# A decoder layer on one core: first weight block, norm tables and block inverse re-ordered

## The chip, the core and the metric

The kernel runs on one core of a Trainium2 chip. The core has TensorE (PE, matrix products, with its weight loads as PEld), VectorE (DVE), ScalarE (ACT), GpSimd (POOL) and SyncE (SP), each with a list of instructions of its own that it works through in order; between engines, semaphores say when an operand is ready. Transfers are issued from the lists of SP, ACT and POOL and carried out by 16 transfer engines. The metric is the device time of one execution in microseconds (us), as the median of several runs.

## The reference

One layer over 256 positions, 2048 channels, all in float32:

```python
h = rmsnorm(x, norm1_g)
qkv, z, b_raw, a_raw, u_raw, v_raw, ga_raw, gb_raw = split(h @ w_in)
# branch A: causal conv + silu on qkv, l2norm of q and k, then the gated delta rule in chunks of 64
L    = strict_lower(k_beta @ k.T * decay)
Tinv = triangular_solve(L + eye, eye)          # per head and chunk, 64 x 64
u = Tinv @ v_beta;  w = Tinv @ (k_beta * exp(g))   # then a scan over 4 chunks with state S
y_a = rmsnorm(o, dn_onorm_g) * silu(z)
# branch B: spatial gating
u  = gelu(u_raw)
vg = layernorm(gelu(v_raw), sg_ln_g, sg_ln_b)
ws = tril(sg_w)                                 # 8 groups of 128 x 128
y_b = u * (ws @ vg + sg_b)
merged = sigmoid(ga_raw) * (y_a @ w_branch_a) + sigmoid(gb_raw) * (y_b @ w_branch_b)
x = x + merged @ w_out
h2 = rmsnorm(x, norm2_g)
x = x + (silu(causal_dwconv(h2 @ ffn_w_gate) + ffn_conv_b) * (h2 @ ffn_w_up)) @ ffn_w_down
out = rmsnorm(x, final_norm_g)
```

## The kernel before

**Dense products.** Every weight matrix is streamed from memory once. A weight block (four slabs of 128 rows by up to 512 columns) is transferred to a `w_raw` buffer, of which there are three. Two slabs at a time, `split` makes a rounded high half `w_hi` (a cast on ACT, L123) and the remainder `w_lo` (a subtraction on DVE, L124); of each half there are four buffers. The activations are held as high and low halves too (`x_h`), and `tok_mms` issues three products per slab and row tile: high by high (L150), high by `w_lo` (L151), low by high (L152). With two row tiles and two slabs a step has twelve products. So PE follows ACT's cast and DVE's subtraction, and they follow PE through the four buffers.

**Stages.** First `vg_pass` computes the columns of v, with input slabs that are scaled and split on the way (L206, L207). Its first block comes in single slabs: g1, x_t and `w_raw` are transferred from SP and ACT. Then the square sums of x (ACT, L318, on tiles `xn`) give the row factors: `rs_v` on DVE (L286), a power on POOL (L287), two diagonal tiles `dg` on DVE, their products `ps_row` on PE (L297), and a copy `rrow` on ACT. In the stage of branch B, ACT applies Gelu to the four v tiles (L337), DVE takes their statistics and normalises them: one instruction per row tile for mean and deviation, and eight half-tile instructions in `affine` for gain and bias. Meanwhile PE computes three groups of u columns (`ps_u`). `sg_w` is loaded as `ws`, masked to its lower triangle on POOL (L382) and transposed on PE (`ps_ws`). Then follow q, k, v, the delta rule of branch A with gates, branch B's projection and z between its steps, the merge, and the feed-forward part, which takes the greater half of the time.

**The order.** The program is a list of operations in Python; generators decide which small operations are written between which dense steps. `affine` yields after each piece, and every second yield lets one dense step of u in. `delta()` yields numbers of dense steps (`fill_steps`: gates, branch B's projection, z), which the loop at the end of the stage takes from the other generator. `inverse_base` solves the 16 by 16 diagonal blocks row by row (L610, L613 on DVE, i from 1 to 15), and yields 2 after every fourth row. A scheduler then places the operations of all engines in an order of its own, by readiness, so that the lists of the engines need not follow the Python order.

Of the kernel before, what the change touches and what calls it, by code (L numbers as in the profile page):

```python
# [16 lines left out]
P = 128  # L17
# [81 lines left out]
def decoder_kernel(ctx: ExitStack, tc: tile.TileContext, a: dict):  # L99
# [15 lines left out]
        return ap.bitcast(F32)  # L115


    def split(raw, shape, tag, dst=None):

        hi, lo = dst or (  # L120
            wsp.tile(shape, F32R, name=f"w_{n}", tag=tag + n)[..., 0 : raw.shape[-1]] for n in ("hi", "lo")
        )
        nc.scalar.copy(hi, raw)  # L123
        nc.vector.tensor_tensor(lo, raw, f32(hi), op=ALU.subtract)  # L124
        return hi, lo

# [107 lines left out]
    def vg_pass():  # L234

        ps = [[bank(pool, "ps_vg") for _ in range(NT)] for pool in (acc, aux)]
        for kb in range(0, NK, 4):
            raws = [wraw.tile([P, 4, 512], F32, name="w_raw", tag="raw") for _ in range(2)]
            n = 2 if kb else 1
            for j in range(0, 4, n):  # L240
                k0 = kb + j
                for c, raw in enumerate(raws):
                    at = P * 512 * (c * NK + kb)
                    block = a["w_vg"][at : at + P * 4 * 512].rearrange("(p k n) -> p k n", p=P, n=512)
                    if k0 == 0 and c == 0:
                        nc.sync.dma_start(g1, a["par"][:, 96:112])
                    if c == 0:
                        queue = nc.sync if k0 else nc.scalar
                        queue.dma_start(x_t[:, k0 : k0 + n, :], a["xt"][:, k0 : k0 + n, :])
                    queue = nc.scalar if k0 == 0 and c else nc.sync  # L250
                    queue.dma_start(raw[:, j : j + n, :], block[:, j : j + n, :])
                if k0 == 0:
                    nc.scalar.copy(tbl, tbl)
                for k in range(k0, k0 + n):
                    split_stat(x_h[:, k, 0:T], x_h[:, k, T:], x_t[:, k, :], g1[:, k : k + 1])
                for c, raw in enumerate(raws):
                    hi, lo = split(raw[:, j : j + n, :], [P, n, 512], "w")
                    tok_mms(ps[c], x_h, NK, k0, n, hi, lo)
        return ps

# [64 lines left out]
    with tc.tile_pool(name="sg", bufs=1) as sg:  # L325
        ln_g = sg.tile([P, SGW], F32, name="ln_g")
        ln_b = sg.tile([P, SGW], F32, name="ln_b")
        nc.gpsimd.dma_start(ln_g, a["sg_ln_g"].partition_broadcast(P))
        nc.gpsimd.dma_start(ln_b, a["sg_ln_b"].partition_broadcast(P))
        vg = sg.tile([P, NT, SGW], F32, name="vg")  # L330
        st = sg.tile([P, NT, 2, 6], F32, name="st")
        ws = sg.tile([P, NG, P], F32, name="ws")
        ws_t = sg.tile([P, NG, P], F32, name="ws_t")
        for c in range(2):
            for t in range(NT):
# [6 lines left out]
            nc.vector.bn_aggr(mv[:, t, :], st[:, t].rearrange("p c s -> p (c s)"))  # L342
        rs = sg.tile([P, NT], F32, name="sg_rs")
        rsqrt_small(rs, mv[:, :, 1], 1.0)
        for t in range(NT):
            nc.vector.tensor_scalar(
                vg[:, t, :], vg[:, t, :], scalar1=mv[:, t, 0:1], scalar2=rs[:, t : t + 1],
                op0=ALU.subtract, op1=ALU.mult,
            )

        def affine():

            for t in range(NT):
                for gain, op in ((ln_g, ALU.mult), (ln_b, ALU.add)):
                    for q in range(2):
                        qs = slice(512 * q, 512 * (q + 1))
                        nc.vector.tensor_tensor(vg[:, t, qs], vg[:, t, qs], gain[:, qs], op=op)
                        yield

        ug = sg.tile([P, NT, SGW], F32, name="ug")  # L360
        for c, (start, width) in enumerate(GROUPS["bau"]):
            steps = tok_steps(x_h, source("bau", c), NK, "ps_u_")
            if c == 0:
                next(steps)
                next(steps)
                for i, _ in enumerate(affine()):
                    if i % 2:
                        next(steps)
            ps = finish(steps)
            n0 = max(0, C_U - start)  # L370
            u0 = start + n0 - C_U
            for t in range(NT):
                if n0:
                    nc.vector.tensor_scalar(
                        ba[:, t], ps[t][:, 0:n0], scalar1=rstd1[:, t : t + 1], scalar2=None, op0=ALU.mult
                    )
                nc.scalar.activation(
                    ug[:, t, u0 : u0 + width - n0], ps[t][:, n0:], AF.Gelu, scale=rstd1[:, t : t + 1]
                )
            if c == 0:  # L380
                nc.gpsimd.dma_start(ws, a["sg_w"].rearrange("g i j -> i g j"))
                nc.gpsimd.affine_select(  # L382
                    ws, ws, pattern=[[0, NG], [-1, P]], compare_op=ALU.is_ge, fill=0.0, base=0, channel_multiplier=1
                )
                for q in range(2):
                    pw = bank(aux, "ps_ws")
                    for g in range(4):
                        nc.tensor.transpose(pw[:, g * P : (g + 1) * P], ws[:, 4 * q + g, :], cm["ident"])
                    nc.scalar.copy(ws_t[:, 4 * q : 4 * q + 4, :], pw.rearrange("p (g i) -> p g i", g=4))
                continue  # L390
            for t in range(NT):
                uh = ug[:, t, 512 * (c - 1) : 512 * c]
                pm = bank(aux, "ps_mix")
                for g in range(4):
                    gg = 4 * (c - 1) + g
                    gs = slice(g * P, (g + 1) * P)
                    nc.tensor.matmul(
                        pm[:, gs], lhsT=ws_t[:, gg, :], rhs=vg[:, t, gg * P : (gg + 1) * P], start=True, stop=True
                    )
                for g in range(4):  # L400
                    gg = 4 * (c - 1) + g
                    gs = slice(g * P, (g + 1) * P)
                    nc.vector.scalar_tensor_tensor(
                        uh[:, gs], pm[:, gs], sgbt[:, gg : gg + 1], uh[:, gs], op0=ALU.add, op1=ALU.mult
                    )
                to_chan(uh, y_b, t, 4 * (c - 1))
# [181 lines left out]
    def inverse_base(lows):  # L588
# [19 lines left out]
        for i in range(1, BASE):  # L608
            pr = dnt.tile([P, 2, BASE, BASE], F32, name="pr", tag="w_sb")[:, :, 0:i, 0:i]
            nc.vector.tensor_tensor(  # L610
                pr, bc(lt[:, :, 0:i, i], 2, i), xs[:, :, 0:i, 0:i].rearrange("p b j c -> p b c j"), op=ALU.mult
            )
            nc.vector.tensor_reduce(xs[:, :, i, 0:i], pr, axis=AX.X, op=ALU.add)  # L613
            if i % 4 == 3:
                yield 2
        res = []
        for n, order in (("x_i", "p b i j -> p j b i"), ("x_it", "p b i j -> p i b j")):
            xc = dnt.tile([P, BASE, 32], F32, name="xc", tag="w_sb")
# [383 lines left out]
```

## Time and profile before

| | |
|---|---|
| runs (median of 3; lowest, highest) | 1433.55 us; 1433.12, 1434.66 |
| profiled execution, its span | 1434.71 us; 1432.8 us |
| PE busy | 1418.1 us (99%) |
| DVE, ACT, POOL busy | 895.9, 718.3, 228.4 us |
| transferred | 269.19 MB, 188 GB/s mean |
| granted clock of TensorE | 0.87 in the first 10 us, 0.95 in the next, then 1.00 |

Times in the rows of a timeline are the start from the span's beginning, then the duration; a row of a group ends with how many instructions it holds, and in brackets stands how long the engine had been idle before it and what ended that. In a row of waits, the engine and its instruction stand left of the arrow, what released it stands right of it, and the numbers are the total, how often, and the longest. The durations of products overlap: the pace is the difference of two starts.

### The profile page before, as it was taken

What the parts mean: (1) busy time and instruction counts of PE and PEld (TensorE: products, weight loads), DVE (VectorE), ACT (ScalarE), POOL (GpSimd) and SP (SyncE); (2) the same over time, 40 slices, a digit from 0 to 9 for tenths busy, and PEclk for the clock granted to TensorE, in tenths of its full rate; (3) what the DMA queues carried; (4) which work ended last, traced back from release to release, by engine and by line L of the source; (5) the groups of instructions that cost most, each with busy time, mean ns of one, the idle gap of its engine ahead of it and who ended that gap; (6) DMA issues with size and microseconds to landing.
All of it is one profiled execution on the core that took longest, in us unless ns stands there. A gap on an engine that the chain in (4) does not pass through costs nothing.

```text
span 1432.8 us, 19529 instructions
## 1 busy us (share of the span) xinstructions
PE 1418.1 (99%) x7768; PEld 1208.2 (84%) x7768; DVE 895.9 (63%) x1121; ACT 718.3 (50%) x977; POOL 228.4 (16%) x216
## 2 busy tenths in 40 slices
PE   9999999999999999999999999999999999999997
PEld 7998888887888888888888888888888888888886
DVE  5666777779465645656566675766766666555555
ACT  6546556543333444445465555555555545444443
POOL 0101111221011200200031221322312221000002
PEclk9999999999999999999999999999999999999999
DMA  7864555545334455575555555555555555555552
GB/s 262 298 216 158 212 191 177 176 147 188 137 120 145 157 196 181 177 286 179 180 183 196 197 185 193 189 183 199 179 204 179 198 183 203 182 202 189 193 199 95
DMA packets 46011, 269.19 MB, mean 188 GB/s; under 512 B 4832, under 2 KB 11744, under 8 KB 16096
## 3 DMA queue, kind: packets, MB, share of 16 engines
q1 hardware_dynamic: 44912, 264.93, 52.5%
q0 software_dynamic: 432, 1.57, 0.4%
q8 instruction: 61, 1.00, 0.3%
q10 hardware_dynamic: 576, 1.44, 0.3%
q14 instruction: 30, 0.25, 0.0%
HBM read 265.83 MB, written 2.10 MB: 187 GB/s over the span
## 4 chain that ended last, share of the span: by engine, by line
PE 90%; DVE 3%; POOL 1%; issue 1%; ACT 0%; POOLq 0%; DVEq 0%
PE ps_gu L183 23%; PE ps_gu L186 11%; PE ps_qkv L183 6%; PE ps_dn L895 5%; PE ps_dn L896 5%; PE ps_dn L894 5%; PE ps_gate L150 4%; PE ps_gate L151 4%; PE ps_gate L152 3%; PE ps_qkv L186 3%; PE ps_wo L150 2%; PE ps_wo L152 2%; PE ps_wo L151 2%; PE ps_br L151 2%; PE ps_br L150 2%; PE ps_br L152 2%
## 5 line engine op out<-in xcount | busy, mean ns | idle before, releaser
L124 DVE TENSOR_TENSOR w_lo<-w_raw,w_hi 128x1024 fp32r<-128x1024 f32 (+3 forms) x412 | 529.7, 1291 | 361.9 <-ACT w_hi L123 359.5
L123 ACT CAST w_hi<-w_raw 128x1024 fp32r<-128x1024 f32 (+3 forms) x412 | 421.9, 1026 | 452.9 <-PE ps_gu L183 156.7
L183 PE MATMUL ps_gu<-x_h,w_hi 128*128 128x512 f32 x1408 | 488.5, 394 | 0.0
L186 PE MATMUL ps_gu<-x_h,w_lo 128*128 128x256 f32 x1408 | 390.3, 277 | 0.0
L183 PEld LDWEIGHTS ps_gu<-x_h,w_hi 128*128 128x128 f32 x1408 | 264.0, 187 | 61.1
L186 PEld LDWEIGHTS ps_gu<-x_h,w_lo 128*128 128x128 f32 x1408 | 264.3, 188 | 0.0
L124 DVE TENSOR_TENSOR w_lo<-wd_raw,w_hi 128x1024 fp32r<-128x1024 f32 x84 | 104.2, 1240 | 105.1 <-ACT w_hi L123 105.1
L123 ACT CAST w_hi<-wd_raw 128x1024 fp32r<-128x1024 f32 x84 | 88.2, 1050 | 120.6 <-PE ps_dn L896 113.3
L183 PE MATMUL ps_qkv<-x_h,w_hi 128*128 128x512 f32 x384 | 133.5, 394 | 0.0
L894 PE MATMUL ps_dn<-w_hi,y_s 128*128 128x512 f32 x336 | 130.7, 389 | 0.0
L896 PE MATMUL ps_dn<-w_hi,y_s 128*128 128x512 f32 x336 | 130.7, 389 | 0.0
L895 PE MATMUL ps_dn<-w_lo,y_s 128*128 128x512 f32 x336 | 130.7, 389 | 0.0
L198 POOL TENSOR_TENSOR gu<-gu,rrow 128x512 f32<-128x512 f32 x44 | 61.4, 1396 | 337.1 <-DVE gu L197 316.0
L186 PE MATMUL ps_qkv<-x_h,w_lo 128*128 128x256 f32 x384 | 106.5, 278 | 0.0
L150 PE MATMUL ps_gate<-w_hi,x_h 128*128 128x512 f32 x256 | 102.1, 399 | 0.0
L151 PE MATMUL ps_gate<-w_lo,x_h 128*128 128x512 f32 x256 | 100.0, 391 | 0.4 <-DVE w_lo L124 0.4
L152 PE MATMUL ps_gate<-w_hi,x_h 128*128 128x512 f32 x256 | 99.8, 390 | 0.0
L183 PEld LDWEIGHTS ps_qkv<-x_h,w_hi 128*128 128x128 f32 x384 | 72.0, 188 | 16.4
L894 PEld LDWEIGHTS ps_dn<-w_hi,y_s 128*128 128x128 f32 x336 | 63.1, 188 | 13.2
L895 PEld LDWEIGHTS ps_dn<-w_lo,y_s 128*128 128x128 f32 x336 | 63.1, 188 | 13.1
L896 PEld LDWEIGHTS ps_dn<-w_hi,y_s 128*128 128x128 f32 x336 | 63.1, 188 | 12.9
L186 PEld LDWEIGHTS ps_qkv<-x_h,w_lo 128*128 128x128 f32 x384 | 72.1, 188 | 0.1
(261 smaller groups left out, 1822.2 us busy)
## 6 DMA issues: line engine op xcount, KB each, us to landing
w_raw<-in_w_gu SPq DMA_DIRECT2D x88, 1024.0 KB, 4.8
wd_raw<-in_ffn_w_down SPq DMA_DIRECT2D x44, 1024.0 KB, 4.8
w_raw<-in_w_qkv SPq DMA_DIRECT2D x24, 1024.0 KB, 4.8
w_raw<-in_w_gb SPq DMA_DIRECT2D x16, 1024.0 KB, 4.8
w_raw<-in_w_ga SPq DMA_DIRECT2D x16, 1024.0 KB, 4.8
w_raw<-in_w_out SPq DMA_DIRECT2D x16, 1024.0 KB, 4.9
w_raw<-in_w_branch_b SPq DMA_DIRECT2D x8, 1024.0 KB, 4.9
w_raw<-in_w_z SPq DMA_DIRECT2D x8, 1024.0 KB, 4.8
```

Source lines behind the costliest of these rows:

```text
L123: nc.scalar.copy(hi, raw)
L124: nc.vector.tensor_tensor(lo, raw, f32(hi), op=ALU.subtract)
L150: nc.tensor.matmul(ps[t], lhsT=xh, rhs=hi[:, j, :], start=(k == 0), stop=False)
L151: nc.tensor.matmul(ps[t], lhsT=xh, rhs=lo[:, j, :], start=False, stop=False)
L152: nc.tensor.matmul(ps[t], lhsT=xl, rhs=hi[:, j, :], start=False, stop=(k == n_k - 1))
L183: nc.tensor.matmul(ps[m], lhsT=hi[:, j, ms], rhs=xk, start=(k == 0), stop=(k == NK - 1), skip_group_check=True)
L186: nc.tensor.matmul(ps[m][:, 0:T], lhsT=lo[:, j, ms], rhs=xk[:, 0:T], start=False, stop=(k == NK - 1), skip_group_check=True,)
L198: nc.gpsimd.tensor_tensor(dst, dst, bc(rrow, 1, 2), op=ALU.mult)
L894: nc.tensor.matmul(o, lhsT=yh, rhs=hi[:, cs], start=(k == 0), stop=False)
L895: nc.tensor.matmul(o, lhsT=yh, rhs=lo[:, cs], start=False, stop=False)
L896: nc.tensor.matmul(o, lhsT=yl, rhs=hi[:, cs], start=False, stop=(k == NF - 1))
```

## The change

There are four edits.

1. In `vg_pass`, the small tensor g1 is issued from ACT's list and no longer from SP's; the second column half of the first slab is issued from SP's list and no longer from ACT's. The first slab of the first half is cast on DVE (`tensor_copy`) and not on ACT.
2. The two norm tables and `sg_w` are issued from ACT's list, one after the other and before the Gelus are written; before, POOL issued them, `sg_w` after the first group of u.
3. All ten pieces of the normalisation (two for mean and deviation, eight for gain and bias, gain and bias now in turn for each half tile) are written between dense steps: five steps of the first group of u, after three without a piece, and five of the second, one piece for each.
4. `inverse_base` yields 2 after rows 3 and 7 as before, and then 1 after each row from 8 to 15, which is eight steps in place of four.

```diff
-    def split(raw, shape, tag, dst=None):
+    def split(raw, shape, tag, dst=None, cast=None):
...
-        nc.scalar.copy(hi, raw)
+        if cast is None:
+            nc.scalar.copy(hi, raw)
+        else:
+            cast.tensor_copy(hi, raw)
         nc.vector.tensor_tensor(lo, raw, f32(hi), op=ALU.subtract)
...
-                    if k0 == 0 and c == 0:
-                        nc.sync.dma_start(g1, a["par"][:, 96:112])
                     if c == 0:
                         queue = nc.sync if k0 else nc.scalar
+                        if k0 == 0:
+                            queue.dma_start(g1, a["par"][:, 96:112])
                         queue.dma_start(x_t[:, k0 : k0 + n, :], a["xt"][:, k0 : k0 + n, :])
-                    queue = nc.scalar if k0 == 0 and c else nc.sync
-                    queue.dma_start(raw[:, j : j + n, :], block[:, j : j + n, :])
+                    nc.sync.dma_start(raw[:, j : j + n, :], block[:, j : j + n, :])
...
-                    hi, lo = split(raw[:, j : j + n, :], [P, n, 512], "w")
+                    hi, lo = split(raw[:, j : j + n, :], [P, n, 512], "w", cast=nc.vector if k0 + c == 0 else None)
...
-        nc.gpsimd.dma_start(ln_g, a["sg_ln_g"].partition_broadcast(P))
-        nc.gpsimd.dma_start(ln_b, a["sg_ln_b"].partition_broadcast(P))
+        nc.scalar.dma_start(ln_g, a["sg_ln_g"].partition_broadcast(P))
+        nc.scalar.dma_start(ln_b, a["sg_ln_b"].partition_broadcast(P))
+        ws = sg.tile([P, NG, P], F32, name="ws")
+        nc.scalar.dma_start(ws, a["sg_w"].rearrange("g i j -> i g j"))
...
-        for t in range(NT):
-            nc.vector.tensor_scalar(
-                vg[:, t, :], vg[:, t, :], scalar1=mv[:, t, 0:1], scalar2=rs[:, t : t + 1],
-                op0=ALU.subtract, op1=ALU.mult,
-            )
-
-        def affine():
+
+        def norm():
 
             for t in range(NT):
-                for gain, op in ((ln_g, ALU.mult), (ln_b, ALU.add)):
-                    for q in range(2):
-                        qs = slice(512 * q, 512 * (q + 1))
-                        nc.vector.tensor_tensor(vg[:, t, qs], vg[:, t, qs], gain[:, qs], op=op)
+                nc.vector.tensor_scalar(
+                    vg[:, t, :], vg[:, t, :], scalar1=mv[:, t, 0:1], scalar2=rs[:, t : t + 1],
+                    op0=ALU.subtract, op1=ALU.mult,
+                )
+                yield
+            for t in range(NT):
+                for q in range(2):
+                    qs = slice(512 * q, 512 * (q + 1))
+                    for tab, op in ((ln_g, ALU.mult), (ln_b, ALU.add)):
+                        nc.vector.tensor_tensor(vg[:, t, qs], vg[:, t, qs], tab[:, qs], op=op)
                         yield
...
-            if c == 0:
+            for _ in range(3 if c == 0 else 0):
                 next(steps)
+            for _ in range((5, 5, 0)[c]):
+                next(pieces)
                 next(steps)
-                for i, _ in enumerate(affine()):
-                    if i % 2:
-                        next(steps)
...
-                nc.gpsimd.dma_start(ws, a["sg_w"].rearrange("g i j -> i g j"))
...
-            if i % 4 == 3:
+            if i in (3, 7):
                 yield 2
+            elif i > 7:
+                yield 1
```

The change moves instructions in the lists of the engines. On PE, the place is the end of v's products (`ps_vg`) and the beginning of u's. Before, its list reads there:

```order
L152 MATMUL ps_vg<-w_hi,x_h 128x512
L150 MATMUL ps_u_514<-w_hi,x_h 128x348
L151 MATMUL ps_u_514<-w_lo,x_h 128x348
...
L297 MATMUL ps_row<-dg,cst 128x128 x2
...
L388 MATMUL ps_ws<-cst,ws 128x128 x8
```

With the change, the same place reads:

```order
L155 MATMUL ps_vg<-w_hi,x_h 128x512
L299 MATMUL ps_row<-dg,cst 128x128 x2
L391 MATMUL ps_ws<-cst,ws 128x128
L153 MATMUL ps_u_513<-w_hi,x_h 128x348
L153 MATMUL ps_u_514<-w_hi,x_h 128x348
L391 MATMUL ps_ws<-cst,ws 128x128 x2
L154 MATMUL ps_u_513<-w_lo,x_h 128x348
```

Before, `ps_row` stood inside the fourth step of u and the eight transposes `ps_ws` after u's first group; now `ps_row` and one transpose stand ahead of u's first product, two more behind its second, and the other five after the group.

On ACT, the place begins at the two square sums of x (`xn`). Before:

```order
L318 ACTIVATE xn,ss_460<-xn 128x2048 x2
L123 CAST w_hi<-w_raw 128x2x348 x6
L337 ACT_TABLE_LOAD
L337 ACTIVATE vg<-ps_vg,rstd_461 128x512 x2
L298 COPY rrow<-ps_row 128x256
```

With the change:

```order
L320 ACTIVATE xn,ss_460<-xn 128x2048 x2
L330 DMA ln_g<-in_sg_ln_g 128x1024
L331 DMA ln_b<-in_sg_ln_b 128x1024
L300 COPY rrow<-ps_row 128x256
L333 DMA ws<-in_sg_w 128x8x128
L340 ACT_TABLE_LOAD
L340 ACTIVATE vg<-ps_vg,rstd_461 128x512 x4
L124 CAST w_hi<-w_raw 128x2x348 x8
```

The six casts of u's weights that stood ahead of the Gelus now stand behind them, and the copy of `ps_row` stands ahead of the issue of `ws`.

On DVE, the place is the end of the block inverse: its last row of sums (`xs`), the transposed blocks `xc`, the tiles `x_i` and `x_it`, and what follows. With the change:

```order
L616 TENSOR_REDUCE xs<-pr 128x2x15
L624 STREAM_TRANSPOSE xc<-xs 128x512 x2
L127 TENSOR_TENSOR w_lo<-w_raw,w_hi 128x1024
L628 TENSOR_TENSOR x_i<-xc,cst 128x512 x2
L127 TENSOR_TENSOR w_lo<-w_raw,w_hi 128x1024
L628 TENSOR_TENSOR x_it<-xc,cst 128x512 x2
L127 TENSOR_TENSOR w_lo<-w_raw,w_hi 128x1024 x5
L775 TENSOR_TENSOR m_b<-ps_br_3198,m_b 128x512
L775 TENSOR_TENSOR m_b<-ps_br_3199,m_b 128x512
L127 TENSOR_TENSOR w_lo<-w_raw,w_hi 128x1024 x4
L646 TENSOR_TENSOR v_b<-ps_vt,bn 128x512 x2
```

Before, the list reads the same, down from the first row of the inverse (with other line numbers), to the two `m_b`; then `v_b` follows at once. The four added dense steps thus stand behind the inverse in this list, as the four subtractions ahead of `v_b`, the first work on what the inverse gives.

More of the change, by code (lines that the diff above doesn't have):

```diff
@@ L327, in decoder_kernel @@
         ln_b = sg.tile([P, SGW], F32, name="ln_b")
-        nc.gpsimd.dma_start(ln_g, a["sg_ln_g"].partition_broadcast(P))
-        nc.gpsimd.dma_start(ln_b, a["sg_ln_b"].partition_broadcast(P))
+        nc.scalar.dma_start(ln_g, a["sg_ln_g"].partition_broadcast(P))
+        nc.scalar.dma_start(ln_b, a["sg_ln_b"].partition_broadcast(P))
+        ws = sg.tile([P, NG, P], F32, name="ws")
+        nc.scalar.dma_start(ws, a["sg_w"].rearrange("g i j -> i g j"))
         vg = sg.tile([P, NT, SGW], F32, name="vg")
         st = sg.tile([P, NT, 2, 6], F32, name="st")
-        ws = sg.tile([P, NG, P], F32, name="ws")
         ws_t = sg.tile([P, NG, P], F32, name="ws_t")
@@ L344, in decoder_kernel @@
         rsqrt_small(rs, mv[:, :, 1], 1.0)
-        for t in range(NT):
-            nc.vector.tensor_scalar(
-                vg[:, t, :], vg[:, t, :], scalar1=mv[:, t, 0:1], scalar2=rs[:, t : t + 1],
-                op0=ALU.subtract, op1=ALU.mult,
-            )
-        def affine():
-            for t in range(NT):
-                for gain, op in ((ln_g, ALU.mult), (ln_b, ALU.add)):
-                    for q in range(2):
-                        qs = slice(512 * q, 512 * (q + 1))
-                        nc.vector.tensor_tensor(vg[:, t, qs], vg[:, t, qs], gain[:, qs], op=op)
+        def norm():
+            for t in range(NT):
+                nc.vector.tensor_scalar(
[8 more added lines that the diff above has]
+                        nc.vector.tensor_tensor(vg[:, t, qs], vg[:, t, qs], tab[:, qs], op=op)
                         yield
+        pieces = norm()
         ug = sg.tile([P, NT, SGW], F32, name="ug")
```

## The prediction

> **What bounds the kernel now.** I read the page first, then the waits of TensorE alone, then the timelines around the three places that the change touches.
>
> ```profile
> PE 1418.1 (99%) x7768; PEld 1208.2 (84%) x7768; DVE 895.9 (63%) x1121; ACT 718.3 (50%) x977; POOL 228.4 (16%) x216
> ...
> PE ps_vg L150 <- ACT w_hi L123: 1.8, 1, 1.8
> PE ps_u L151 <- DVE w_lo L124: 1.7, 1, 1.7
> PE ps_wup L219 <- POOL neg_half L272: 1.0, 1, 1.0
> PE ps_br L151 <- DVE w_lo L124: 0.7, 3, 0.3
> PE ps_gate L151 <- DVE w_lo L124: 0.4, 1, 0.4
> ```
>
> TensorE (PE) is busy for 1418.1 of 1432.8 us. Its waits are 5.6 us in all, and they are all that a better order can win. A new wait of PE, on the other hand, costs its full length, since nothing later has slack to take it back. So the question is where PE stands still afterwards.
>
> The three edits aim at three rows here: the first weights at the start (1.8), the wait for the low half of u's weights beside the normalisation (1.7), and the four waits in the block inverse (1.1).
>
> **The start.** The first real product begins at 6.28:
>
> ```profile
> 6.28 0.73 PE L150 MATMUL ps_vg<-w_hi,x_h 128*128 128x512 f32 x2 [1.81 <-ACT w_hi L123]
> ...
> 9.35 0.63 PE L151 MATMUL ps_vg<-w_lo,x_h 128*128 128x512 f32 x1
> 9.78 0.63 PE L152 MATMUL ps_vg<-w_hi,x_h 128*128 128x512 f32 x1
> ...
> 10.99 0.39 PE L150 MATMUL ps_vg<-w_hi,x_h 128*128 128x512 f32 x1
> 11.22 0.40 PE L151 MATMUL ps_vg<-w_lo,x_h 128*128 128x512 f32 x1
> ```
>
> The weights' transfer moves to the front of SP's queue, so the cast can begin between 0.5 us (one issue less ahead of it) and 1.2 us earlier (a transfer that no longer shares with its neighbour). VectorE (DVE) also gets one instruction more ahead of the low half of x. I take 0.6 us, between 0 and 1.2. It will turn out that the end does not see it. These rows carry a price for later: from 6.28 to about 10.6 the products start 0.43 us apart, from 10.99 on 0.23.
>
> **The hand-over from vg to u.** Here the change costs most, and it is not the line that the diff shows: the order in which the engines' work stands has changed. Before, ScalarE (ACT) cast six blocks of u ahead of the Gelus, and PE went on without a gap:
>
> ```profile
> 51.84 0.32 PE L150 MATMUL ps_u<-w_hi,x_h 128*128 128x348 f32 x1
> ...
> 57.76 0.32 PE L150 MATMUL ps_u<-w_hi,x_h 128*128 128x348 f32 x1
> 58.00 0.71 PE L297 MATMUL ps_row<-dg,cst 128*128 128x128 f32 x4
> 58.47 0.40 PE L151 MATMUL ps_u<-w_lo,x_h 128*128 128x348 f32 x1
> ```
>
> Now PE's list has ps_row and then one ps_ws transpose ahead of u's first product, and ACT's list has the copy of ps_row, the issue of ws, the table load and four Gelus ahead of u's first cast. Two chains decide when PE goes on. Both hang on the second square sum, after which DVE starts rs_v (timelines of DVE, POOL and ACT; columns: start, duration):
>
> ```profile
> 50.51 0.17 DVE L286 TENSOR_SCALAR rs_v<-ss 128x2 f32<-128x2 f32 x1 [7.04 <-ACT xn L318]
> ...
> 51.67 0.97 POOL L287 TENSOR_TENSOR rstd<-rs_v,neg_half 128x2 f32<-128x2 f32 x1
> ...
> 56.06 0.77 ACT L123 CAST w_hi<-w_raw 128x696 fp32r<-128x696 f32 x1 [1.13 <-PE ps_u L152]
> 56.85 1.28 ACT L337 ACT_TABLE_LOAD   x1
> ...
> 57.66 0.48 DVE L294 TENSOR_SCALAR dg<-cst,rstd 128x128 f32<-128x128 f32 x2
> 58.14 1.26 ACT L337 ACTIVATE vg<-ps_vg,rstd 128x512 f32<-128x512 f32 x2
> 59.30 0.37 ACT L298 COPY rrow<-ps_row 128x256 f32<-128x256 f32 x1
> 59.55 1.29 ACT L337 ACTIVATE vg<-ps_vg,rstd 128x512 f32<-128x512 f32 x2
> ```
>
> First chain, through ACT. rs_v is there at 50.7. The power on GpSimd (POOL) takes 0.97 and starts at once, as POOL issues no table now: 51.7. The two diagonals take 0.48 (52.3), ps_row 0.71 (53.0), its copy 0.37 (53.4), the issue of ws 0.4 (53.8; the issues on ACT's queue at the start take 0.39 to 0.41), the table load 1.28 (55.1), the four Gelus 2.55 (57.6), the cast 0.77: 58.4. So u cannot start before 58.4, whatever the transfers do.
>
> Second chain, through ws. Its transfer is issued at about 53.4, behind the copy, and POOL masks it before PE may transpose it. The rows are POOL's mask, three groups of transfers (KB each, us from issue to landing) and a window whose last three numbers are granted clock, share of the transfer engines and GB/s:
>
> ```profile
> 61.43 1.10 POOL L382 TENSOR_SCALAR_AFFINE_SELECT ws<-ws 128x1024 f32<-128x1024 f32 x1 [7.32 <-DMA ws<-in_sg_w]
> ...
> w_raw<-in_w_bau SPq DMA_DIRECT2D x4, 696.0 KB, 10.5
> ...
> out<-x ACTq DMA_DIRECT2D x2, 512.0 KB, 2.8
> ...
> ws<-in_sg_w POOLq DMA_DIRECT2D x1, 512.0 KB, 8.2
> ...
> 50.00:62.00 12.00, 12.00 (x72) 11.19 (x71) 8.37 (x14) 9.14 (x15) 3.79 (x5) 1.00 0.94 306
> ```
>
> The same bytes took 8.2 us from POOL's queue (landed by 61.43) and 2.8 us is what as many bytes take on ACT's queue at the kernel's end, with nothing beside them. So the landing lies between 56.2 and 61.6. From 50 to 62 us the transfer engines are 94% busy at 306 GB/s, so the bytes in line decide, not the issuer. One thing leaves the line: the fourth block of u's weights (696 KB) needs a buffer that u's first subtractions free, and these now come behind the Gelus. 0.70 MB at 306 GB/s is 2.3 us: 61.4 - 2.3 = 59.1. I take that. It is nearer the upper bound because the engines are as busy as there. With 1.1 for the mask and 0.2 for the hand-overs PE goes on at 60.4.
>
> Here the Trainium skill ("DMA: Bandwidth & Descriptors", section "Queues, rings and completion order") says that each transfer engine takes turns between the queues that have work, packet by packet. By this rule ws, last of three tables on ACT's queue, lands near the end of all that is queued, as in my sum. By the 2.8 us row alone PE would go on at 58.4, two us sooner.
>
> The terms, against 51.84 before: +8.6 (60.4). ps_row no longer stands inside u: before, the step from 57.76 to 58.47 took 0.71 instead of 0.17, so -0.5.
>
> **The clock.** Between ps_row (53.0) and 60.4 PE has nothing for 7.4 us. The longest gap of a running PE in this trace is the one at u, and there the pace was full at once:
>
> ```profile
> 73.29 0.43 PE L151 MATMUL ps_u<-w_lo,x_h 128*128 128x346 f32 x1 [1.69 <-DVE w_lo L124]
> 73.55 0.32 PE L152 MATMUL ps_u<-w_hi,x_h 128*128 128x346 f32 x1
> 73.72 0.32 PE L150 MATMUL ps_u<-w_hi,x_h 128*128 128x346 f32 x1
> ```
>
> 7.4 us is over four times that gap, and after the start's idle time the products ran at 0.43 instead of 0.23 for 4.3 us. If the slow pace comes back, it costs 4.3 x (1 - 0.23/0.43) = 2.0 us; the bounds are 0 and 3. I take 2.0, because no gap of this length in the trace has gone without it.
>
> The Trainium skill ("TensorE: Matmul & The Clock Gate", section "What's actually happening") states that an idle window of about 3.4 us halves the clock and that about 3.4 us of work restores it. By this rule the loss would be some 1.7 us by estimate, by the 1.69 us gap alone nothing. The start's rows agree with the halving; no run here yet shows a long gap in the middle.
>
> **The normalisation.** The pieces now stand between the subtractions (DVE order: a subtraction, a piece or two, a subtraction). PE also starts u with three subtractions already done.
>
> ```profile
> 54.96 0.88 DVE L124 TENSOR_TENSOR w_lo<-w_raw,w_hi 128x696 fp32r<-128x696 f32 x1 [0.37 <-ACT w_hi L123]
> ...
> 67.26 1.29 DVE L357 TENSOR_TENSOR vg<-vg,ln_g 128x512 f32<-128x512 f32 x2
> ```
>
> Per step DVE needs 0.88 and 1.29 for two pieces (2.2), PE 2.0 (twelve products 0.17 apart, as from 73.55 to 73.72). The pieces fall in six of eight steps, so DVE loses at most about 1 us on PE over u's first group, and it is three steps ahead. The wait of 1.69 disappears: -1.7. If that lead is not there, it stays: 0.
>
> **The block inverse.** Its yields change, yet DVE's list from the first small product to the x_it tiles is the same, row for row. The waits come from this stretch of DVE:
>
> ```profile
> 339.40 1.19 DVE L124 TENSOR_TENSOR w_lo<-w_raw,w_hi 128x1024 fp32r<-128x1024 f32 x1
> 340.51 2.13 DVE L623 TENSOR_TENSOR x_i<-xc,cst 128x512 f32<-128x512 f32 x2
> ```
>
> Two tiles and a subtraction take 3.3 us while PE needs 2.7 for twelve products 0.23 apart; that pattern is unchanged, so 0 (bounds -1.0, all four waits gone, and 0). What moves is what comes after: the work on the finished inverse (ps_vt, ps_w and on) begins 48 dense products, four steps, later on PE, and at the chain's end so many fewer stand beside it. There the state update is the longest piece of DVE work:
>
> ```profile
> 457.77 2.16 DVE L714 SCALAR_TENSOR_TENSOR s_st<-s_st,egl,ps_d 128x128 f32<-128x128 f32 x8 [1.44 <-PE ps_d L704]
> ```
>
> Its eight parts (0.27 each) go head by head, and the products that read them come in the same order, so I count 0, at worst +1.
>
> **The sum.** +8.6 - 0.5 - 1.7 + 2.0 + 0 = +8.4. Against the profiled execution (1434.71, of which 1432.8 is the span) that is 1443.1. The median of the runs shown is 1433.55, 1.2 below it, so the forecast of the median is 1441.9. The start's 0.6 is not in it: PE only arrives earlier at the gate.
>
> **The rivals.** For a measurement of this kernel 0.2% (2.9 us) is about no change.
>
> 1. The gate is as above but the clock does not fall, or ws lands at 56.2 so that the first chain (58.4) decides with the slow clock. Either way +6.4: 1439.9. For it: the 1.69 us gap at full pace, and the 2.8 us row. Against: the length of the gap, and 94% busy transfer engines. 25%.
> 2. More than I count: ws takes 8.2 us (PE at 62.9, +2.5) and the delta chain's end waits 1: +11.9, so 1445.4. For it: the same transfer took that long. Against: one block fewer in line. 13%.
> 3. The gate costs nothing and the edits do what they aim at: 0.6 at the start, 1.7 beside the normalisation, 1.0 in the inverse, so -3.3: 1430.2. Its one mechanism is an earlier square sum. u's first cast is 7.9 us behind the sum, so it decides only if the sum is there by 44, not 50.5, since u must start at 51.8. For it: a queue that starts 0.5 to 1.2 us earlier. Against: x's tiles land at 46 and 48 with the transfer engines full, and the start's gain is a fifth of what is needed. 5%.
> 4. The gate is half as long, and the gains nearly pay for it: +2, 1435.5. It needs a sum 2 us earlier and no slow clock. 6%.
>
> The forecast itself has 51%. Its bounds come from the unknown terms: 1436.7 with 58.4, a full clock and no waits in the inverse (+3.2), 1447.8 with 62.9, a clock loss of 3, the wait at u kept and +1 at the chain's end (+14.2). Ends as extreme as these need all terms on one side, so the range goes from 1436.5 to 1446.5 and leaves out rival 3, most of rival 4 and the last of rival 2. Faster by over 0.2% is 5%, within 0.2% 6%, slower 89%.
>
> **What would show it.** PE's waits in the profile after: one at ps_ws, released by POOL's mask, of about 7 us, starting near 53; a first u cast at or after 57.5; TensorE's granted clock below 1.00 in the stretch after 60; no wait of 1.7 us in u; four waits of some 1.0 us still in the inverse. Wrong would be: a u product before 58, a gate released by ACT's cast instead of the mask (then the landing was overrated), a granted clock of 1.00 throughout, or waits of over 2 us beside the delta chain.

## The result, and the profile after

The changed kernel takes 1443.98 us in the median (1440.98 to 1445.59, four runs), the kernel before 1434.11 beside it (1433.12 to 1434.96). The ratio is 1.0067 with a 95% interval of 1.0047 to 1.0087, so +9.6 us, between 6.7 and 12.5. The forecast was 1441.9, within 1436.5 to 1446.5. The sign and the main cause were right. One part of the loss was forecast at nothing, and it is the more instructive one.

In the page of the kernel after, the busy row and the waits of TensorE (us in total, times, longest):

```profile
PE 1422.1 (99%) x7768; PEld 1212.6 (84%) x7768; DVE 898.3 (62%) x1122; ACT 718.0 (50%) x976; POOL 225.4 (16%) x213
...
PE ps_ws L391 <- POOL ws L385: 7.8, 1, 7.8
PE ps_vg L153 <- ACT x_h L209: 1.4, 1, 1.4
PE ps_s L682 <- DVE s_st L719: 1.0, 1, 1.0
...
PE ps_br L154 <- DVE w_lo L127: 0.5, 2, 0.3
PE ps_gate L154 <- DVE w_lo L127: 0.4, 1, 0.4
```

The wait for POOL's mask is there, 7.8 us long. The wait of 1.7 in u is gone. The inverse's waits still come to 0.9 (0.5 and 0.4, before 1.1). One wait is new and was not forecast: ps_s waits 1.0 for the state update s_st.

Where the time comes from is read by laying the starts of the same products side by side. First qkv's first product, the first product of the delta chain and wo's first product, in the kernel before:

```profile
104.89 0.48 PE L183 MATMUL ps_qkv<-x_h,w_hi 128*128 128x512 f32 x1
...
239.98 0.73 PE L513 MATMUL ps_g<-gl,cst 128*128 128x8 f32 x6
...
603.49 0.47 PE L150 MATMUL ps_wo<-w_hi,x_m 128*128 128x512 f32 x1
```

and in the kernel after:

```profile
112.62 0.48 PE L186 MATMUL ps_qkv<-x_h,w_hi 128*128 128x512 f32 x1
...
247.71 0.73 PE L516 MATMUL ps_g<-gl,cst 128*128 128x8 f32 x6
...
614.18 0.47 PE L153 MATMUL ps_wo<-w_hi,x_m 128*128 128x512 f32 x1
```

The differences are 7.73, 7.73 and 10.69 us. So 7.7 us arise before qkv and 3.0 between the delta chain's start and wo; elsewhere nothing changes. The spans differ by 10.6 (1443.4 against 1432.8).

**The hand-over.** PE's timeline after (start, duration):

```profile
51.75 0.61 PE L299 MATMUL ps_row<-dg,cst 128*128 128x128 f32 x4
60.12 0.47 PE L391 MATMUL ps_ws<-cst,ws 128*128 128x128 f32 x1 [7.76 <-POOL ws L385]
60.25 0.93 PE L153 MATMUL ps_u<-w_hi,x_h 128*128 128x348 f32 x2
...
64.59 0.49 PE L154 MATMUL ps_u<-w_lo,x_h 128*128 128x348 f32 x1
64.88 0.38 PE L155 MATMUL ps_u<-w_hi,x_h 128*128 128x348 f32 x1
65.09 0.32 PE L153 MATMUL ps_u<-w_hi,x_h 128*128 128x348 f32 x1
65.25 0.32 PE L154 MATMUL ps_u<-w_lo,x_h 128*128 128x348 f32 x1
```

POOL's mask, which releases it, and ACT's list at the same place:

```profile
58.94 1.12 POOL L385 TENSOR_SCALAR_AFFINE_SELECT ws<-ws 128x1024 f32<-128x1024 f32 x1 [8.03 <-DMA ws<-in_sg_w]
```

```profile
52.40 0.39 ACTq L333 DMA_DIRECT2D ws<-in_sg_w  x1
52.82 1.28 ACT L340 ACT_TABLE_LOAD   x1
54.12 2.42 ACT L340 ACTIVATE vg<-ps_vg,rstd 128x512 f32<-128x512 f32 x4
56.41 2.80 ACT L124 CAST w_hi<-w_raw 128x696 fp32r<-128x696 f32 x4
```

A window of the same stretch (its last three numbers are the granted clock of TensorE, the busy share of the transfer engines and GB/s), and the rate of the transfers from 48 to 60 us in 40 slices of 0.3 us:

```profile
56.00:64.00 8.00, 3.88 (x14) 3.82 (x15) 7.13 (x12) 3.21 (x5) 2.42 (x2) 0.50 0.37 114
...
GB/s 394 390 404 403 376 394 403 353 325 255 303 421 397 388 256 319 397 324 378 278 152 209 211 251 326 358 306 217 145 79 48 24 22 22 12 0 0 0 0 0
```

u begins at 60.25, 8.4 us late. ws is issued at 52.4 and masked from 58.94 on; ACT's first cast would have been ready at about 57.2. The transfers fall below 100 GB/s at 56.7 and stop at 58.5, so most of the bytes are through two us before the mask can begin. The granted clock is 0.50 from 56 to 64. Up to 64.6 the products start 0.29 apart, from 65.1 on 0.16: by the sixteenth product the lateness has grown from 8.41 to 10.66, so the slow pace costs about 2.25 (two ws transposes now stand among these products and have a small part in it). Afterwards it falls back to 7.7: ps_row and some of the ws transposes no longer stand inside u (0.6 and 0.3), the wait of 1.7 is absent, and 0.3 comes from the place of the small ps_mix products.

**The end of the delta chain.** PE after, at the last step of the recurrence:

```profile
464.83 1.96 PE L699 MATMUL ps_u<-v_b,x_it 64*64 64x128 f32 x16
466.72 0.50 PE L153 MATMUL ps_gate<-w_hi,x_h 128*128 128x512 f32 x1
467.06 0.39 PE L154 MATMUL ps_gate<-w_lo,x_h 128*128 128x512 f32 x1
467.38 2.05 PE L709 MATMUL ps_d<-v_b,k_d 64*128 64x128 f32 x16
470.45 2.00 PE L682 MATMUL ps_s<-s_st,kq 128*128 128x128 f32 x10 [1.02 <-DVE s_st L719]
```

Before, 24 products of z stood ahead of this ps_u, 24 between it and ps_d, and 12 between ps_d and ps_s. Now 12, none and none are left, and two products of gate. Those are the 48 that the inverse's finer steps took earlier. DVE and POOL beside it:

```profile
465.06 4.96 DVE L127 TENSOR_TENSOR w_lo<-w_raw,w_hi 128x1024 fp32r<-128x1024 f32 x2
470.05 2.16 DVE L719 SCALAR_TENSOR_TENSOR s_st<-s_st,egl,ps_d 128x128 f32<-128x128 f32 x8
```

```profile
465.70 3.24 POOL L807 TENSOR_TENSOR v_t<-v_t,zs 128x1024 f32<-128x1024 f32 x1
468.89 2.26 POOL L786 TENSOR_TENSOR zs<-zs,on_g 128x512 f32<-128x512 f32 x1
```

Two subtractions stand ahead of the update on DVE, and they take 4.96 us where 1.2 each is usual. In the windows, the granted clock then falls (the third number from the end):

```profile
470.00:472.00 2.00, 1.55 (x9) 1.55 (x10) 1.97 (x9) 0.00 (x0) 1.14 (x1) 0.79 0.41 90
472.00:474.00 2.00, 2.00 (x10) 1.81 (x9) 1.94 (x6) 0.00 (x0) 0.00 (x0) 0.50 0.98 410
474.00:476.00 2.00, 2.00 (x9) 1.17 (x8) 1.46 (x6) 0.00 (x0) 0.00 (x0) 0.85 0.06 25
```

From this I formed theory A: two losses, one at the hand-over made by the tables on ACT's queue, one at the chain's end made by the inverse's steps. The experiments test each by itself.

### The profile page after: what moved, and what is told of

It reads as the page before. It is cut to its first block, busy times and chain, and to the rows that moved or that the text cites. A ratio compares the mean times of both kernels' runs of the same rounds, so it can differ in the third digit from the quotient of the medians.

```text
span 1443.4 us, 19522 instructions
## 1 busy us (share of the span) xinstructions
PE 1422.1 (99%) x7768; PEld 1212.6 (84%) x7768; DVE 898.3 (62%) x1122; ACT 718.0 (50%) x976; POOL 225.4 (16%) x213
## 4 chain that ended last, share of the span: by engine, by line
PE 94%; DVE 3%; DMA 1%; issue 1%; POOL 1%; ACT 0%; POOLq 0%; ACTq 0%; DVEq 0%
PE ps_gu L186 23%; PE ps_gu L189 11%; PE ps_qkv L186 6%; PE ps_dn L900 5%; PE ps_dn L901 5%; PE ps_dn L899 5%; PE ps_gate L153 4%; PE ps_gate L155 4%; PE ps_gate L154 3%; PE ps_qkv L189 3%; PE ps_wo L155 2%; PE ps_wo L153 2%; PE ps_wo L154 2%; PE ps_br L153 2%; PE ps_br L154 2%; PE ps_br L155 2%
```

## The experiments

Every kernel ran beside the kernel before on its chip. Times are given as the difference to that one, from the ratio and its 95% interval (0.001 is 1.43 us).

### One thing undone

ws back on POOL's queue, behind u's first group; all else as after:

```diff
...
-        nc.scalar.dma_start(ws, a["sg_w"].rearrange("g i j -> i g j"))
...
             if c == 0:
+                nc.gpsimd.dma_start(ws, a["sg_w"].rearrange("g i j -> i g j"))
```

> The kernel after, with one thing undone: ws is issued from POOL behind u's first group again, as before; the two norm tables stay on ACT's queue. In PE's list u's products then stand directly behind vg, and ACT casts six blocks of u ahead of the Gelus. Theory A (the hand-over's loss is the wait for ws plus the slow clock that it brings, 8.4 + 2.3 us, and a second loss of 3.0 us sits at the end of the delta chain, made by the inverse's finer steps): u starts between 52 and 53.5, clock 1.00 there, the wait of 1.0 us before ps_s at the chain's end stays, and the time is 1434.1 - 1.7 (normalisation) - 0.5 to +1 (two issues ahead of the first cast) + 3.0 = 1435 to 1437. Rival B (ACT's chain through the Gelus decides the hand-over whatever ws does): u starts at 57.4 and the clock still falls: 1441.

Measured: ratio 0.9983 (0.9974 to 0.9992), so -2.4 us (-3.7 to -1.1): faster than the kernel before, where I had expected +1 to +3. The trace agrees with A on the mechanism, and rival B falls. u's first product starts at 51.78 without a wait, and the granted clock there is 1.00. ACT's chain through the Gelus does not gate by itself, since without the early ws the casts stand ahead of the Gelus again. qkv begins 1.4 us earlier than before, and the chain's end then costs 1.5, not 3.0, so the two spans are alike (1432.7 and 1432.8). The runs of the kernel before range from 1431.6 to 1439.1 beside it, those of ws_back from 1432.3 to 1434.5; what it avoids in the longer ones is not in these traces.

The inverse's old yields, all else as after:

```diff
-            if i in (3, 7):
+            if i % 4 == 3:
                 yield 2
-            elif i > 7:
-                yield 1
```

> The kernel after with the inverse's old yields (2 after every fourth column); all else stays. Theory A (the finer yields spend 48 dense products earlier, so that the chain's end stands bare; 1.0 us of waiting and 1.8 us of slow clock there): the wait before ps_s and the clock of 0.50 near 472 go, 1444.0 - 3.0 = 1441.0. Rival C (as predicted, the yields cost nothing and the 3 us come from something that only runs later because u is late): the time stays at 1444.

Measured: 1.0039 (1.0027 to 1.0051), so +5.6 (3.9 to 7.3), against +9.6 (6.7 to 12.5) for the whole change. The two were measured on different runs and their intervals meet, so the trace decides. There the wait before ps_s and the slow pace at the chain's end are gone: wo begins 7.49 us later than before, against 10.69. Rival C, which was my prediction, falls.

### One edit alone

The new yields put into the kernel before, twice:

```diff
-            if i % 4 == 3:
+            if i in (3, 7):
                 yield 2
+            elif i > 7:
+                yield 1
```

> The kernel before with the new yields of the inverse and nothing else. Theory A: the chain's end loses its cover, +3.0: 1437.1, with a wait of about 1 us before ps_s and a granted clock of about 0.5 for some 3 us near 462. Rival C: 1433.1 to 1434.1, with no new wait.

> The kernel of inverse_alone once more, beside inverse_quiet. Theory A: the wait of 1.0 before ps_s stands in this trace too, and the chain's end comes 1.5 us later against the products before it if the granted clock stays at 1.00 there, about 3 if it falls as in the kernel after. Rival: the end's loss differs from execution to execution with no such two values.

Measured: 1.0004 (0.9992 to 1.0015) and 1.0011 (1.0001 to 1.0022), so +0.6 and +1.6 us, each less than the 3.0 expected. The traces say why: the loss has two values. From the delta chain's first product to wo's the lateness grows by 1.5 in the first trace, by 3.0 in the second. Both have the wait of 1.0 before ps_s. Only the second has the slow pace. The windows of the second, and those of ws_back, which has the same wait at the same place and a growth of 1.5:

```profile
466.00:468.00 2.00, 2.00 (x12) 1.90 (x11) 1.97 (x8) 0.00 (x0) 0.22 (x1) 0.57 0.99 270
468.00:470.00 2.00, 2.00 (x10) 1.51 (x9) 1.47 (x5) 0.00 (x0) 0.00 (x0) 0.58 0.60 254
```

```profile
461.00:463.00 2.00, 1.57 (x11) 1.55 (x12) 1.97 (x8) 0.00 (x0) 1.12 (x1) 1.00 0.42 94
463.00:465.00 2.00, 2.00 (x13) 1.39 (x11) 1.94 (x6) 0.00 (x0) 0.00 (x0) 1.00 0.92 389
```

Over the six traces with this chain's end (the kernel after, inverse_again, inverse_alone, ws_back, ws_early, early_filled), the growth is 2.96, 2.96, 1.52, 1.51, 1.51 and 1.45. So the end costs 1.5, plus another 1.5 where the clock falls. The profiled execution of the kernel after had the fall; in four of the six traces the finer yields cost 1.5 and not 3.

The three tables on ACT's queue, alone:

```diff
-        nc.gpsimd.dma_start(ln_g, ...)
-        nc.gpsimd.dma_start(ln_b, ...)
+        nc.scalar.dma_start(ln_g, ...)
+        nc.scalar.dma_start(ln_b, ...)
+        nc.scalar.dma_start(ws, ...)
...
-                nc.gpsimd.dma_start(ws, ...)
```

> The kernel before with one edit: ln_g, ln_b and ws issued on ACT's queue, ws at once behind the tables. The order turns as in the kernel after: ps_row and three ps_ws transposes ahead of u's first product, the Gelus ahead of u's first cast. Theory A (the whole hand-over loss is this edit's): u goes on at about 60, the granted clock is 0.5 for some 4 to 5 us behind it, +8.4 + 2.3 - 0.6 (ps_row and transposes no longer inside u) = +10 over the kernel before of the same runs; the delta chain's end as before. Rival (the edit needs the others, the norm pieces above all, to lose): below +5.

Measured: 1.0058 (1.0043 to 1.0072), so +8.3 (6.2 to 10.3). This one edit makes nearly the whole loss of the hand-over: in its trace qkv begins 7.1 us later than in the kernel before, against 7.7 with all four edits. PE waits 6.9 us for POOL's mask and u begins at 59.78. A detail answers a question of the prediction: ACT issued ws at 49.41 here, 3.0 us before the kernel after did (52.40), yet the mask began only 0.9 earlier (58.08 against 58.94). So the moment of the issue counts for little where transfers stand in line. The bytes in line are not all of it either: from 56 to 58 us the transfer engines move 1 GB/s in this trace, and the mask still waits for ws until 58.08. What holds its last part is open. The wait of 1.7 in u is absent too, without any norm pieces: a late u alone removes it.

The norm pieces alone, twice:

```diff
...
-            if c == 0:
+            for _ in range(3 if c == 0 else 0):
                 next(steps)
+            for _ in range((5, 5, 0)[c]):
+                next(pieces)
                 next(steps)
-                for i, _ in enumerate(affine()):
-                    if i % 2:
-                        next(steps)
```

> The kernel before with the norm pieces bound to ten dense steps and nothing else (tables and ws still on POOL's queue, u first behind vg). Theory A: the wait of 1.7 us for w_lo in u goes and nothing takes its place: 1434.1 - 1.7 = 1432.4. Rival D: that wait was not DVE's order but the start of the normalisation itself, which then is late for ps_mix: 1433.5 to 1434.5, with a wait at ps_mix or at the second group of u.

> The kernel of norm_alone once more, since its first interval held both -1.4 and no change. Theory A: the pieces take the wait of 1.7 us out of u and nothing else changes: 0.998 to 0.9995 of the kernel before. Rival D: no change on the whole, 1.000 and above, since the wait comes back elsewhere in some executions; then the trace shows a wait in u or at ps_mix. If qkv runs at 175 products in 30 us here, and not 172 as in the first trace, that pace belongs to the execution and not to the edit.

Measured: 0.9991 (0.9980 to 1.0002) and 0.9992 (0.9981 to 1.0003), so -1.3 and -1.1 us. Each interval still holds no change; the two agree with each other and come near the 1.7 of the wait. In both traces the wait in u is gone and nothing replaces it there. That qkv ran at the lower count of products in both is taken up below.

### The hand-over taken apart

ws in a place of its own, loaded at the kernel's start:

```diff
+    ws_ctx = ExitStack()
+    ws = ws_ctx.enter_context(tc.tile_pool(name="wse", bufs=1)).tile([P, NG, P], F32, name="ws")
+    nc.gpsimd.dma_start(ws, a["sg_w"].rearrange("g i j -> i g j"))
     x_ctx = ExitStack()
...
-        ws = sg.tile([P, NG, P], F32, name="ws")
-        nc.scalar.dma_start(ws, a["sg_w"].rearrange("g i j -> i g j"))
...
+    ws_ctx.close()
```

> The kernel after, but ws has a place of its own and is issued on POOL's queue at the kernel's start, so that its mask is long done at the hand-over. PE's list: ps_row, all eight ps_ws transposes, then u; ACT's list: copy of ps_row, table load, four Gelus, then u's first cast. Theory A (two chains, ws the longer by 2.9 us): u's first product is released by ACT's cast at 57.0 to 57.5, a gap of about 4 us; +5.5 for the gate. The clock: if a gap of 4 us is long enough, 0.5 for some 4 us (+2), else 1.00. Normalisation -1.7, ps_row and transposes -1.0, chain's end +1.5 to +3: in all +4.5 to +8 over before. Rival (ws is the only gate, ACT's chain hides): u at 53 to 54, and no more than +1 to +3.

The same with 40 small products that keep PE busy until u (only the added loop; `ps_r` is the tile that ps_row fills):

```diff
...
+    for _ in range(40):
+        nc.tensor.matmul(ps_r[0:64, 256:320], lhsT=rrow[:, 0:64], rhs=rrow[:, 0:64], start=True, stop=True)
```

> As ws_early, with 40 small products of no use on PE between the transposes and u (64x64, input the copy of ps_row), which keep PE busy through the gap. Theory A (clock loss is a cost of its own beside the waiting): u's first product still at about 57.2 to 57.8, granted clock 1.00 behind it, u's products 0.16 apart from the first on: 1.5 to 2.3 us faster than ws_early. Rival (slow pace behind the gap comes from late weights, not from the clock): the products stay 0.29 apart and the time is that of ws_early.

Measured: 1.0050 (1.0038 to 1.0063) and 1.0044 (1.0031 to 1.0057), so +7.2 and +6.3. The first shows the chain through ACT: u's first product is released by ACT's cast after a wait of 3.7, at 59.47. That is 2 us later than I expected, since the second square sum ends at 52.4 instead of 49.9. The early load does not explain that, since early_filled has the same load and its sum ends at 50.5; why it is late here is open. In both, u's first cast is ready 7.0 us behind that sum. So moving ws early takes the gate from POOL's mask and leaves it with ACT's chain, and the rival falls. The windows of the first, then of the filled one:

```profile
58.00:60.00 2.00, 0.53 (x2) 0.30 (x2) 2.00 (x5) 2.00 (x5) 0.00 (x0) 1.00 0.04 16
60.00:62.00 2.00, 1.62 (x7) 1.57 (x7) 2.00 (x5) 2.00 (x5) 0.54 (x1) 0.66 0.00 0
62.00:64.00 2.00, 2.00 (x9) 2.00 (x8) 1.41 (x3) 0.81 (x2) 0.67 (x1) 0.50 0.64 159
```

```profile
56.00:58.00 2.00, 2.00 (x35) 1.93 (x33) 2.00 (x5) 2.00 (x5) 0.00 (x0) 1.00 0.00 0
58.00:60.00 2.00, 1.88 (x11) 1.63 (x12) 2.00 (x5) 1.94 (x4) 0.52 (x1) 1.00 0.00 0
```

With PE kept busy the granted clock stays at 1.00 and u's products start 0.16 apart almost from the first, beginning at 57.90. In this pair of traces the slow pace is thus a price of PE's idleness and not of late weights. From u's start to qkv the filled kernel makes up 1.35 us more than the other. The end-to-end times differ only by 0.9, within their intervals, so the 1.35 rests on the traces alone. The two spans (1440.6 and 1440.5) do not show it: in the filled trace qkv takes 2.5 us longer, which is taken up at the end.

### The chain's end taken apart

The kernel of the new yields alone, with POOL's work there left out (so the gain on one block of z and the product of one token tile's output with z are not computed):

```diff
-                nc.gpsimd.tensor_tensor(h128(o), h128(o), bc(on_g, 1, 4), op=ALU.mult)
+                if c == 0:
+                    nc.gpsimd.tensor_tensor(h128(o), h128(o), bc(on_g, 1, 4), op=ALU.mult)
...
-            nc.gpsimd.tensor_tensor(o, o, zs[:, c].rearrange("p (h d) -> p h d", h=H), op=ALU.mult)
+            if c:
+                nc.gpsimd.tensor_tensor(o, o, zs[:, c].rearrange("p (h d) -> p h d", h=H), op=ALU.mult)
```

> The kernel of inverse_alone with POOL idle at the chain's end: it leaves out the norm gain on the second block of z and the product of the first token tile's output with z, so two parts of the result are not computed. PE's and DVE's order there is that of inverse_alone. Theory E (the chain's end waits because POOL's multiplications stretch the two subtractions that stand ahead of the state update on DVE, 4.95 us for the pair instead of 2.45): the pair takes 2.45, the update starts as soon as ps_d is there, and the wait of 1.0 before ps_s falls to 0 to 0.3; some 1.0 us below inverse_alone. Rival F (the bare chain ps_d, update, ps_s has that latency whatever DVE does before): the wait stays at about 1.0.

Measured: 0.9999 (0.9989 to 1.0010), so -0.1 (-1.6 to 1.4). This interval meets those of inverse_alone and inverse_again, so the trace has to decide. DVE, then PE, at the same place:

```profile
459.45 1.23 DVE L124 TENSOR_TENSOR w_lo<-w_raw,w_hi 128x1024 fp32r<-128x1024 f32 x1
460.98 1.23 DVE L124 TENSOR_TENSOR w_lo<-w_raw,w_hi 128x1024 fp32r<-128x1024 f32 x1 [0.30 <-ACT w_hi L123]
462.97 1.12 DVE L716 SCALAR_TENSOR_TENSOR s_st<-s_st,egl,ps_d 128x128 f32<-128x128 f32 x4 [0.76 <-PE ps_d L706]
```

```profile
461.77 2.05 PE L706 MATMUL ps_d<-v_b,k_d 64*128 64x128 f32 x16
463.75 1.38 PE L679 MATMUL ps_s<-s_st,kq 128*128 128x128 f32 x10
```

The pair takes 1.23 each, DVE now waits for ps_d instead of the reverse, and ps_s follows ps_d without a wait. The lateness grows by 0.24 instead of 1.5 or 3.0. Theory E holds in this trace, and rival F falls. The bare chain alone costs a quarter of a microsecond; what costs is that POOL and DVE collide there. The Trainium skill ("SBUF — State Buffer", section "Who interferes with whom") states that a DVE instruction with two inputs in SBUF contends with a POOL instruction that reads SBUF, and that what they share, a pair of ports, is locked exclusively. The trace agrees: 4.96 for the pair against 1.23 each, and POOL's product takes 3.24 beside it where it took 2.36 in the kernel before.

### Two versions beyond

The kernel after, with ws back on POOL and the inverse's old number of dense steps (of the single yields only those after rows 9, 11, 13 and 15 are left, so these steps are still spread more finely than before):

> The kernel after with ws back on POOL behind u's first group and the inverse's old number of dense steps (its DVE and PE order is then that of before); the start's edit, the norm pieces and the tables on ACT's queue stay. Theory A: normalisation -1.4 as the trace of norm_alone and ws_back show, start 0, no gate, no bare chain's end: -1.5 to -3.5 over the kernel before of the same runs, about 1.5 below ws_back. Rival (the norm pieces gain nothing by themselves): 0.

Measured: 0.9987 (0.9978 to 0.9996), so -1.9 (-3.2 to -0.6). It is faster than both kernels, but not than ws_back, although it lacks the four added steps that cost 1.5 there; the two intervals meet. In its trace vg ended 1.7 us earlier than before, and then PE waited 1.5 for u's first cast. The two table issues stand between the square sum and that cast on ACT and make 0.9 of it. What the quicker start of this execution had won was lost there, and the slow pace came on top: qkv begins 0.2 later than in the kernel before, where ws_back's began 1.4 earlier. In these two traces that is the 1.5 which I had expected below ws_back and which did not come; whether it is so in the other executions is not shown:

```profile
51.80 0.59 PE L153 MATMUL ps_u<-w_hi,x_h 128*128 128x348 f32 x2 [1.50 <-ACT w_hi L124]
```

```profile
52.00:54.00 2.00, 1.67 (x7) 1.38 (x7) 2.00 (x3) 1.77 (x3) 0.27 (x1) 0.77 1.02 259
54.00:56.00 2.00, 2.00 (x8) 2.00 (x8) 1.04 (x2) 0.26 (x1) 0.00 (x0) 0.50 1.02 295
56.00:58.00 2.00, 2.00 (x12) 2.00 (x12) 1.28 (x3) 0.52 (x1) 0.00 (x0) 0.88 0.95 300
```

The kernel before with the start's edit and the norm pieces, all tables on POOL:

> The kernel before with the start's edit and the norm pieces, all three tables on POOL's queue and the inverse as before. Theory A: no wait of 1.7 us in u, no issue on ACT's queue between the square sums and u's first cast, so PE has no wait at u's first product even when vg ends early; -1.4 us and, if the start gains, down to -2: 1 us or so below two_edits at best. Rival (the start's edit costs, since x's first part lands later): as norm_alone or above, with a wait of 1.5 to 2.1 for x_h at the first product.

Measured: 1.0016 (1.0007 to 1.0025), so +2.3 (1.0 to 3.6). Neither the theory nor the rival had this size. The start waits for x_h as the rival said, but 3.6 us arise later, in u: ACT's list now holds seven casts ahead of the Gelus instead of six, and the seventh waits 4.9 us for its weights to land:

```profile
61.59 0.78 ACT L124 CAST w_hi<-w_raw 128x696 fp32r<-128x696 f32 x1 [4.86 <-DMA w_raw<-in_w_bau]
```

So the Gelus begin at 63.7, where they began at 58.1 in the kernel before and at 56.4 in norm_alone. Behind them PE waits 1.2 for a cast and 0.5 and 1.6 for subtractions, with a granted clock of 0.54 between 68 and 70. What the norm pieces win is lost where ACT's list is held up at this place.

## Why the prediction was right, and where it was not

- **The gate, +8.6.** Measured +8.4 (u at 60.25, forecast 60.4). PE is released by POOL's mask, which starts at 58.94 where the forecast had the landing at 59.1. That ws is the gate, and nearer the 8.2 us row than the 2.8, was right, and tables_alone bears it out. That the landing came so near is luck in part. The sum took 0.70 MB out of the line. From 50 us to the mask the transfer engines moved 302 GB/s x 11.43 us = 3.5 MB before and 232 GB/s x 8.94 us = 2.1 MB after, so 1.4 MB left it. At the sum's 306 GB/s that alone would give a landing at about 56.9, and there the rate does fall (79 GB/s from 56.7 on); but the last part of ws landed two us later, and the two errors cancel. The first chain was put at 58.4 and stood at 57.2, since the square sum came 0.6 earlier and ws's issue ran beside the copy; so the first cast began at 56.4, not at or after 57.5 as the list of signs had it.
- **ps_row out of u, -0.5.** Measured -0.6. The transposes, another -0.3, were not counted.
- **The clock, +2.0.** Right: 2.25 in the trace, and early_filled shows that it hangs on PE's idleness. The size was taken from the start's rows, and a gap that long had not been seen.
- **The normalisation, -1.7.** The wait is gone. But the sum credits the pieces, and tables_alone shows that a late u removes it without them. Alone they are worth about 1.2.
- **The start, not felt at the end.** Right for another reason: it won nothing. The first product waits for x_h now, as x's first part lands 4.2 us after its issue in the kernel after and 2.4 in the kernel before, and it begins at 6.09 to 6.47 in the seven traces with the edit, against 5.87 to 6.51 in the seven without.
- **The inverse, 0.** The step that failed is "Its eight parts (0.27 each) go head by head, and the products that read them come in the same order, so I count 0, at worst +1". It looked at the update's own duration and at DVE's order. It did not ask what stands ahead of the update on DVE once the cover is gone, nor what POOL does then. The term is 3.0 in the profiled execution and 1.5 where the clock does not fall. Of the 1.5 the collision with POOL is all but 0.24 (inverse_quiet); that the fall of the clock follows from the wait that the collision makes is argued from where it stands, not shown.

- **The rivals.** An early ws or a full clock (rival 1), no gate (3) and half a gate (4) did not come. The result lies between the forecast and rival 2, whose extra at the chain's end was the right place with too small a price.
- **The sum.** By their own terms its two extremes come to +3.4 and +14.6, not +3.2 and +14.2. That moves them to 1436.9 and 1448.1, and the range hardly hangs on it.

So the forecast was 2.1 us below the result. Up to qkv it said +8.4 and 7.7 came in the profiled execution; behind it, it said 0 and 3.0 came.

## What to carry to other kernels

When work is moved under a chain, count what is left beside the chain's end, and lay all engines that run there side by side: the cover that is gone lets two other engines' work meet. A DMA moved to a compute engine's queue cost less here by its issue than by what the order of the lists made of it: one load that looks early can pull its consumers ahead of the main work. Price a new wait of PE with the slow pace behind it.

## What the runs showed that I had not expected

Short waits of PE bring the slow pace too, in some executions. The wait of 1.0 before ps_s did in two of six traces, the wait of 1.5 in two_edits did, and the granted clock also fell behind those of 1.2 and 0.5 in start_and_norm, though the wait of 1.7 in the kernel before did not bring it. The Trainium skill ("TensorE: Matmul & The Clock Gate", section "What's actually happening") speaks of an idle window of about 3.4 us, free-running. It gives as much for the recovery. On the recovery the traces agree at these short waits: at half pace, the windows of the kernel after make 0.84 + 2.0 + 0.60 = 3.4 us at the chain's end, and those of inverse_again and two_edits 3.4 each. Behind the long gap of the hand-over the half pace went on for 4.7 us after u's first product (60.25 to 65.0). On the idle time they differ, since these waits are a third to less than a half of it. The small products around the chain's end may count for less than full activity; that was not tried.

The stage of qkv has two paces. In 30 us PE starts 175 products in eight of the fourteen traces and 171 or 172 in six, at a granted clock of 1.00 in all of them. The kernels of inverse_alone and inverse_again are the same program; their windows, one after the other:

```profile
150.00:180.00 30.00, 30.00 (x175) 26.25 (x174) 24.51 (x37) 18.52 (x30) 6.00 (x6) 1.00 0.51 177
```

```profile
150.00:180.00 30.00, 30.00 (x172) 26.03 (x171) 22.76 (x36) 18.25 (x30) 5.00 (x5) 1.00 0.53 185
```

Over the whole stage this is 2.5 us, as much as most of the effects here. It is not made by an edit of the code, and its cause stays open. The start has two paces as well: vg ended 1.6 to 2.0 us earlier than in the kernel before in three of the fourteen traces, with the first products 0.23 instead of 0.43 apart. So two traces are worth comparing only stage by stage, and an effect of 2 us needs many runs: the kernel before ranged from 1431.6 to 1439.4 over the later ones.
